# One fused VectorE instruction per head for distance and row maximum, and a single PSUM bank for the values, in the attention of a two-layer encoder

## The chip, the core and the metric

The kernel runs on one core of one Trainium2 chip. The metric is the device time of one execution in microseconds (us). A core has five engines, each with an instruction queue of its own, worked through in order: TensorE (PE: matmuls and transposes, results to the accumulator memory PSUM; PEld is its loading of the stationary operand), VectorE (DVE), ScalarE (ACT), GpSimd (POOL) and SyncE (SP, which here issues most of the DMAs). They meet through semaphores. PSUM has eight banks of 128 partitions x 512 fp32 numbers.

## The reference

Two layers, each of feed-forward, mixer, feed-forward, with a residual and a LayerNorm behind each; the mixer of the first layer is an mLSTM, that of the second the attention that the change touches. 256 tokens, width 1024, 16 query heads of 64 in 4 groups that share keys and values.

```python
def window_attention(x, w_in, sink, w_out):
    """GQA where each query sees keys with |t-s| <= WINDOW, ALiBi bias, per-head sink logit; banded blocks."""
    ...
    s = jnp.einsum('bnqkgd,bnskd->bnkgqs', q, kw).astype(jnp.float32) * (HEAD_DIM ** -0.5)
    ...
    s = s - slopes[:, :, None, None] * dist
    s = jnp.where(valid[None, :, None, None], s, MASK_VALUE)
    ...
    m = jnp.maximum(jnp.max(s, axis=-1, keepdims=True), sink_l)
    pe = jnp.exp(s - m)
    attn = pe / (jnp.sum(pe, axis=-1, keepdims=True) + jnp.exp(sink_l - m))
    o = jnp.einsum('bnkgqs,bnskd->bnqkgd', attn, vw.astype(jnp.float32)).reshape(B, S, nq)
    return o.astype(x.dtype) @ w_out
```

## The kernel before

**Numbers in two parts.** Every operand of a matmul is held as two tiles, hi (rounded to the type fp32r) and lo (the rest). A product is three matmuls, hi x hi, hi x lo and lo x hi (`mm3`, L467). The hi part is made by ScalarE, the lo part by VectorE, for weights (`w_hi`, `w_lo`) as for results that leave PSUM (`split_evac`).

**Weights.** `Weights` (L141) holds a plan of weight pieces in the order of their use. Raw pieces of 512 KB are loaded by SP into four buffers; `high` casts one (ScalarE), `low` subtracts (VectorE) and then loads the next into the buffer that came free. In the attention the call `W.done(..., PU[st], True)` lets at most `PU[st]` pieces be cast in stage `st`, and `W.lows()` makes their low parts.

**Order.** Nothing is reordered (`manual_schedule`): each engine gets its instructions in the order of the Python code. Each instruction of PE, DVE and ACT is recorded by one helper, so that they all show as L132 in the profile and are told apart by the names of their tiles.

**The attention** (`attn`, L1083). POOL first fills constants, zeroes `kp` and computes `dist`, the distance of each query and key (1e33 outside the window). The projections of keys, values and the first queries follow (`proj`, `k_turn`, `q_turn`); the remaining queries are 32 small steps (`q_rest`). Queries are scaled by 1/slope of their head, so scores and distance have one scale. Then eight pairs of heads j go through a pipeline of eleven stages `st` (L1277):

- `scores(j)` in stage j, for each half t of the queries: three matmuls of 512 columns (two heads x 256 keys) and a fourth that adds -1 x `dist`, into one PSUM bank; VectorE takes the row maxima of both heads in one `reduce_max` (`rm`). Then `nm` = -slope x `rm`, and the smaller of that and -sink. ScalarE takes four exponentials from PSUM (`sc`), each with its row sum (an instruction that reads the accumulator follows each), and two small ones of the sink (`es`).
- `scale(j)` in stage j+1, on POOL: the normaliser (a sum, a power of -1) and four scalings of `sc`.
- `turn(j, 0)` and `turn(j, 1)` in stage j+2: four transposes each into a bank, ScalarE's copy `pr_hi`, and later (`flush`) VectorE's `pr_lo`. In stages 2 to 7 the second turn stands behind the matmuls of `scores`.
- `values(j)` in stage j+3: the stationary operand is the two parts of the values side by side, 64 + 64 columns; four matmuls of 512 columns, so that each half of the partitions holds one part's product. ScalarE copies two quarters of the bank (`o`), VectorE adds the other two, and `qT[j]` takes the sum (`q_hi`, `q_lo`).
- What else PE has to do (`fill`): in stages 0 to 3 the steps of `q_rest` between the entries of `QC`, in stages 4 to 10 the output projection `out_proj(st - 4)`, at the end of the stage.

Four PSUM banks (`pw`) serve scores, turns and values in turn; the second turn of a stage uses the bank that the stage's `values` had. Behind the loop the output projection of pair 7 and of the second half of the tokens follows (`tail`), and LayerNorm.

Of the kernel before, what the change touches and what calls it, by code (L numbers as in the profile page):

```python
# [9 lines left out]
F32 = mybir.dt.float32  # L10
FR = mybir.dt.float32r
# [14 lines left out]
S_RAW = 6  # L26
V_RAW = 2
RING = 10
PU = [3, 1, 2, 1, 1, 1, 1, 1, 0, 1, 1, 2]
QC = [5, 16, 22, 27, 32]  # L30
SW = 1
CT = [0, 1]
LC = [1, 0, 0, 0, 0, 1]
TD = [0, 3, 2, 0, 2, 2]
# [280 lines left out]
def trunk_kernel(ctx: ExitStack, tc: tile.TileContext, x, ffn_w_in, ffn_w_out, ln_g, ln_b, ml_w_in, ml_gate_b,  # L315
# [151 lines left out]
    def mm3(o, l, r, start, stop, onto=False):  # L467
        nc.tensor.matmul(o, l[0], r[0], start=start, stop=False, skip_group_check=onto)
        nc.tensor.matmul(o, l[0], r[1], start=False, stop=False, skip_group_check=onto)
        nc.tensor.matmul(o, l[1], r[0], start=False, stop=stop, skip_group_check=onto)  # L470

    def pair(p, *idx):
        return p[0][idx], p[1][idx]
# [9 lines left out]
    def tok(t):  # L483
        return slice(t * 128, (t + 1) * 128)

    def split_evac(dst, src, scale=None):
        if scale is None:
            nc.scalar.copy(dst[0], src)
            nc.vector.tensor_sub(dst[1], src, dst[0].bitcast(F32))
        else:  # L490
            nc.scalar.activation(dst[0], src, AF.Copy, scale=scale)
            nc.vector.scalar_tensor_tensor(dst[1], src, scale, dst[0].bitcast(F32), op0=OP.mult, op1=OP.subtract)
# [590 lines left out]
    def attn(l, n, pending, last):  # L1083
        with ExitStack() as ph:
# [3 lines left out]
            def both(shape, name, bufs=1):  # L1088
                return tuple(tile_(shape, FR, name + e, bufs=bufs) for e in ("_hi", "_lo"))

            minus_one = tile_([128, 32], F32, "minus_one")[:, 0:4].rearrange("p (t a) -> p t a", t=2)
            nc.gpsimd.memset(minus_one, -1.0)
            slope = [2.0 ** (-(h + 1) / 2) for h in range(16)]
            neg_slope = tile_([128, 16], F32, "neg_slope")
            for h in range(16):
                nc.gpsimd.memset(neg_slope[:, h:h + 1], -slope[h])
            qs_row = tile_([128, 8], F32, "qs_row")
            qs_col = tile_([128, 4], F32, "qs_col")
            for h in range(8):
# [7 lines left out]
            for d, sign in ((fwd, 1), (back, -1)):  # L1107
# [4 lines left out]
                                        channel_multiplier=sign)  # L1112
                nc.gpsimd.affine_select(d, d, pattern=[[-128 * sign, 2], [sign, S]], compare_op=OP.is_ge, fill=1e33,
                                        base=128, channel_multiplier=-sign)
            dist = tile_([128, 2, S], FR, "dist")
            nc.gpsimd.tensor_add(dist, fwd, back)
            va = [tile_([128, 4, 2, 64], FR, f"v{t}") for t in range(2)]
            qT = both([128, 8, S], "q")
            kd, qd = [], []

# [2 lines left out]
            def proj(t, m):  # L1123
                ps = wbank()
                for k in range(8):
                    if t == 0 and m == 1 and k == PEND[bound[0] - 1]:
                        pending()
                        W.done(0, PD[bound[0] - 1])
                    if 4 * m + k // 2 == len(pieces):
                        pieces.extend(W.take(1))  # L1130
                    mm3(ps, pair(xT, A, k, tok(t)), pair(pieces[4 * m + k // 2], A, k % 2), k == 0, k == 7)
                    if t == 1 and k % 2:
                        W.done(W.used - 8 + 4 * m + k // 2 + 1, 1 if m == 0 and k < 4 else 0)
                if m == 0:
                    kv = ps.rearrange("p (a g d) -> p a g d", a=2, g=4)
                    kk = tile_([128, 4, 2, 64], F32, "kd", tag="sc", bufs=6)
                    nc.scalar.copy(kk, kv[:, 0, :, None, :].to_broadcast([128, 4, 2, 64]))
                    split_evac((va[t][:, :, 0], va[t][:, :, 1]), kv[:, 1])
                    kd.append(kk)
                else:  # L1140
                    qq = tile_([128, 4, 128], F32, "qd", tag="sc", bufs=6)
                    nc.vector.tensor_mul(qq.rearrange("p j (a d) -> p (j a) d", a=2),
                                         ps.rearrange("p (h d) -> p h d", h=8),
                                         qs_row[:, :, None].to_broadcast([128, 8, 64]))
                    qd.append(qq)
# [39 lines left out]
            def scores(j, between):  # L1185
                g = j // 2
                rm = tile_([128, 2, 2], F32, "rm", bufs=3)
                nm = tile_([128, 2, 2], F32, "nm", bufs=3)
                sm = tile_([128, 2, 2], F32, "sm", bufs=3)
                es = tile_([128, 2, 2], F32, "es", bufs=3)  # L1190
                wide_ = lambda v: v[:, None, 2 * j:2 * j + 2].to_broadcast([128, 2, 2])
                if SW:
                    p1 = wbank((128, 2, S))
                    ps = [wbank((128, 2, S)), p1]
                else:
                    ps = [wbank((128, 2, S)), wbank((128, 2, S))]
                for t in range(2):
                    p = ps[t]
                    mm3(p, pair(qT, A, j, tok(t)), pair(kp, A, g), True, False)
                    nc.tensor.matmul(p, neg_id, dist[:, t, None, :].to_broadcast([128, 2, S]), start=False, stop=True)  # L1200
                    nc.vector.reduce_max(rm[:, t], p, axis=AX.X)
                nc.vector.tensor_mul(nm, rm, wide_(neg_slope))
                nc.vector.tensor_tensor(nm, nm, wide_(neg_sink), op=OP.min)
                if between is not None:
                    between()
                for t in range(2):
                    s_ = tile_([128, 2, S], F32, "sc", bufs=6)
                    for a in range(2):
                        nc.scalar.activation(s_[:, a], ps[t][:, a], AF.Exp, bias=nm[:, t, a:a + 1],
                                             scale=slope[2 * j + a], accum_out=sm[:, t, a:a + 1])  # L1210
                    sc[j, t] = s_
                for a in range(2):
                    nc.scalar.activation(es[:, :, a], nm[:, :, a], AF.Exp, bias=sink[:, 2 * j + a:2 * j + a + 1])
                stat[j] = sm, es
# [19 lines left out]
            lows, sums = [], {}  # L1234

            def values(j):
                p = wbank((128, 2, S))
                for e in range(2):
                    for sb in range(2):
                        v = va[sb][:, j // 2].rearrange("p a d -> p (a d)")  # L1240
                        nc.tensor.matmul(p, v, pr[j, sb][e], start=e == sb == 0, stop=e == sb == 1)
                o = tile_([128, S], F32, "o", bufs=2)
                top, low = slice(0, 64), slice(64, 128)
                nc.scalar.copy(o[top], p[top, 0])
                nc.scalar.copy(o[low], p[low, 1])
                nc.vector.tensor_add(o[top], p[low, 0], o[top])
                nc.vector.tensor_add(o[low], p[top, 1], o[low])
                sums[j] = o

            y = []  # L1250

            wo = {}

            def out_proj(c, toks):
                if not y:
                    y.extend([ybank() for _ in range(2)] for _ in range(2))
                if c not in wo:
                    wo[c], = W.take_rows(1)
                for t in toks:
                    for o in range(2):  # L1260
                        mm3(y[t][o], pair(qT, A, c, tok(t)), pair(wo[c][1], A, 0, slice(o * 512, o * 512 + 512)),
                            c == 0, False)

            proj(0, 0)
            proj(0, 1)
# [11 lines left out]
            for st in range(11):  # L1277
                if st == 2:
                    gb = load_ln(lambda name: tile_([128, D], F32, name), l, n)
                if 0 <= st - 3 < 8:  # L1280
                    values(st - 3)
                if 0 <= st - 1 < 8:
                    scale(st - 1)
                late = None
                if 0 <= st - 2 < 8:
                    p0, p1 = wbank((128, 2, S)), wbank((128, 2, S))
                    turn(st - 2, 0, p0)
                    late = lambda: turn(st - 2, 1, p1)
                    if st >= 8 or not SW:
                        late()  # L1290
                        late = None
                if 0 <= st - 3 < 8:
                    o = sums.pop(st - 3)
                    d = pair(qT, A, st - 3)
                    nc.scalar.copy(d[0], o)
                    lows.append((d, o))
                held = [wo[c][0] for c in wo if c not in CT]
                W.done(min([W.used - (2 if qpart else 0)] + held), PU[st], True)
                if st < 8:
                    scores(st, late)  # L1300
                flush(3)
                W.lows()
                if st in fill:
                    f_, *args = fill[st]
                    f_(*args)
            nc.scalar.preload_act_table(AF.Silu)
            W.done(0, PU[11])
            wo[7], = W.take_rows(1)
# [46 lines left out]
```

## Time and profile before

| | us |
|---|---|
| median of 3 runs | 941.51 (940.34 to 942.21) |
| the profiled execution | 940.93 |
| its span, first to last instruction | 939.2 |
| PE busy | 923.1 (98%) |
| DVE busy | 800.5 (85%) |
| ACT busy | 546.6 (58%) |
| the loop over pairs of heads, about | 685 to 744 |

TensorE's granted clock is 0.999 of full speed. Matmuls are pipelined: a row's duration (0.39 us for 512 columns) is longer than the step from one start to the next (0.227 us), so TensorE can show as busy while it waits a little. A row of the groups reads: line, engine, operation, output<-inputs by name, partitions x elements and type, count | busy us, mean ns of one | idle time of the engine just before them, and what ended most of it.

### The profile page before, as it was taken

Reading aid. Unit: us, or ns where it says so; the run is one execution under the profiler, and the core shown is the slowest. Engines: PE = TensorE matmul, PEld = TensorE weight load, DVE = VectorE, ACT = ScalarE, POOL = GpSimd, SP = SyncE. Lnnn points to the kernel's source line nnn. Section 1 sums busy time; section 2 is a strip of 40 time slices with the busy share of each in tenths; the row PEclk is TensorE's granted clock in tenths of the full one; section 3 lists DMA queues with packets and bytes.
Section 4 is the critical chain, followed back from the end, with each engine's and each line's share of the span. In section 5 each row is a group of like instructions: output and inputs, shape, how many; then the busy total and the mean of one; then the engine's idle time right before and its main releaser. Section 6 shows DMA issues by size and latency. Waiting matters only on the chain.

```text
span 939.2 us, 12338 instructions
## 1 busy us (share of the span) xinstructions
PE 923.1 (98%) x4416; PEld 765.2 (81%) x4416; DVE 800.5 (85%) x943; ACT 546.6 (58%) x781; POOL 103.2 (11%) x162
## 2 busy tenths in 40 slices
PE   8999999999999999999999999999999999999996
PEld 7888888889878788888888888887887788888885
DVE  6899998787697799988888899977878888898975
ACT  5666756347563548565535566563678554757460
POOL 2010101011111000101010101010545300000100
PEclk9999999999999999999999999999999999999999
DMA  8979764546434949695559597746543266769531
GB/s 277 353 189 326 224 225 89 203 134 219 163 119 145 311 143 336 170 323 135 174 160 347 126 326 210 247 90 201 178 141 109 68 223 248 229 219 311 162 87 45
DMA packets 98461, 187.54 MB, mean 200 GB/s; under 512 B 6720, under 2 KB 37456, under 8 KB 98400
## 3 DMA queue, kind: packets, MB, share of 16 engines
q1 hardware_dynamic: 91648, 174.09, 53.7%
q0 software_dynamic: 6752, 12.66, 8.3%
q8 instruction: 35, 0.57, 0.2%
q14 instruction: 26, 0.21, 0.1%
HBM read 185.68 MB, written 1.05 MB: 199 GB/s over the span
## 4 chain that ended last, share of the span: by engine, by line
PE 84%; DVE 7%; ACT 3%; DMA 2%; issue 2%; POOL 1%; SPq 1%; DVEq 0%; ACTq 0%
PE pw L132 55%; PE py L132 29%; DVE w_lo L132 2%; DMA s_raw<-in_ffn_w_in_dram 1%; ACT w_hi L132 1%; DMA w_raw<-in_ffn_w_in_dram 1%; ACT sc L132 1%; DVE h L132 1%; DVE x L132 1%; DMA w_raw<-in_ml_w_in_dram 0%; SPq L98 0%; DVE o L132 0%; DVE rm L132 0%; DVE pr_lo L132 0%; DVE wt L132 0%
## 5 line engine op out<-in xcount | busy, mean ns | idle before, releaser
L132 DVE TENSOR_TENSOR w_lo<-w_raw,w_hi 128x1024 fp32r<-128x1024 f32 (+1 forms) x237 | 280.8, 1216 | 17.6 <-ACT w_hi L132 15.5
L132 ACT CAST w_hi<-w_raw 128x1024 fp32r<-128x1024 f32 (+1 forms) x237 | 240.6, 1049 | 72.9 <-DMA w_raw<-in_ffn_w_in_dram 21.7
L132 PE MATMUL pw<-w_hi,xT_hi 128*128 128x512 f32 x560 | 222.4, 397 | 0.3 <-ACT xT_hi L132 0.3
L132 PE MATMUL pw<-w_hi,xT_lo 128*128 128x512 f32 x560 | 218.8, 391 | 0.0
L132 PE MATMUL pw<-w_lo,xT_hi 128*128 128x512 f32 x560 | 218.2, 390 | 0.1
L132 ACT CAST w_hi<-s_raw 128x1024 fp32r<-128x1024 f32 x144 | 148.3, 1051 | 92.2 <-DVE s_raw L132 56.4
L132 DVE TENSOR_TENSOR w_lo<-s_raw,w_hi 128x1024 fp32r<-128x1024 f32 x144 | 172.6, 1219 | 21.4 <-ACT w_hi L132 21.3
L132 PE MATMUL py<-w_hi,h_hi 128*128 128x512 f32 x352 | 138.1, 392 | 0.3 <-ACT h_hi L132 0.3
L132 PE MATMUL py<-w_hi,h_lo 128*128 128x512 f32 x352 | 137.3, 390 | 0.2 <-DVE h_lo L132 0.2
L132 PE MATMUL py<-w_lo,h_hi 128*128 128x512 f32 x352 | 137.1, 390 | 0.0
L132 PEld LDWEIGHTS pw<-w_hi,xT_lo 128*128 128x128 f32 x560 | 105.1, 188 | 23.3 <-DVE xT_lo L132 0.8
L132 PEld LDWEIGHTS pw<-w_lo,xT_hi 128*128 128x128 f32 x560 | 105.3, 188 | 20.8 <-DVE w_lo L132 0.4
L132 PEld LDWEIGHTS pw<-w_hi,xT_hi 128*128 128x128 f32 x560 | 105.2, 188 | 20.7 <-ACT xT_hi L132 0.7
L132 DVE TENSOR_TENSOR s_raw<-s_raw 128x1024 f32<-128x1024 f32 x72 | 87.0, 1219 | 0.7
L261 POOL DMA_DIRECT2D s_raw<-in_ffn_w_in_dram x24 | 29.0, 1209 | 496.4 <-DVE w_lo L132 378.3
L132 PEld LDWEIGHTS py<-w_hi,h_lo 128*128 128x128 f32 x352 | 66.1, 188 | 15.1 <-DVE h_lo L132 1.4
L132 PEld LDWEIGHTS py<-w_hi,h_hi 128*128 128x128 f32 x352 | 66.1, 188 | 13.9 <-ACT h_hi L132 0.7
L132 PEld LDWEIGHTS py<-w_lo,h_hi 128*128 128x128 f32 x352 | 66.1, 188 | 13.7 <-DVE w_lo L132 0.4
L132 PE MATMUL pw<-w_hi,S_hi 128*128 128x512 f32 x192 | 74.7, 389 | 0.0
L132 PE MATMUL pw<-w_hi,S_lo 128*128 128x512 f32 x192 | 74.7, 389 | 0.0
L132 PE MATMUL pw<-w_lo,S_hi 128*128 128x512 f32 x192 | 74.7, 389 | 0.0
L132 DVE TENSOR_TENSOR h_lo<-pw,h_hi 128x512 fp32r<-128x512 f32 x44 | 30.2, 687 | 23.3 <-ACT h_hi L132 23.0
(218 smaller groups left out, 1114.1 us busy)
## 6 DMA issues: line engine op xcount, KB each, us to landing
w_raw<-in_ffn_w_out_dram SPq DMA_DIRECT2D x88, 512.0 KB, 5.3
s_raw<-in_ffn_w_in_dram SPq DMA_DIRECT2D x72, 512.0 KB, 6.0
w_raw<-in_ffn_w_in_dram SPq DMA_DIRECT2D x56, 512.0 KB, 5.0
w_raw<-in_ffn_w_in_dram SPq DMA_DIRECT2D x96, 256.0 KB, 4.4
s_raw<-in_ffn_w_in_dram POOLq DMA_DIRECT2D x24, 512.0 KB, 5.9
w_raw<-in_ml_w_in_dram SPq DMA_DIRECT2D x24, 512.0 KB, 4.5
w_raw<-in_at_w_in_dram SPq DMA_DIRECT2D x12, 512.0 KB, 4.5
w_raw<-in_ml_w_out_dram SPq DMA_DIRECT2D x8, 512.0 KB, 3.6
```

Of the source, the lines that this page charges most:

```text
L132: r = f(out, *args, **kw)
L261: nc.gpsimd.dma_start(t.rearrange("p (k f) -> p k f", k=self.words[w]["k"]), v, accum_op=OP.add)
```

## The change

The distance leaves the matmuls. `scores` has three matmuls of 512 columns per half; then, for each head, one VectorE instruction reads the scores from PSUM and `dist` from SBUF, writes their difference to `sc` in SBUF, and takes its row maximum, which starts from sink/slope (`sink_max`, made by POOL), so that the separate minimum with -sink goes. In the built program each such instruction is followed by one that reads its accumulator into `rm`. The exponentials read `sc` and not PSUM. Between the halves of the queries one waiting `pr_lo` is made (`flush(1)`).

The values lie between zeros: a tile has five columns of 64 per group (zero, hi, zero, lo, zero), filled by POOL beforehand. A window of 128 columns that begins on a zero column or on a part puts one head's product into the upper or the lower half of the partitions and zero into the other, so both heads, both token blocks and the three products hi x hi, lo x hi and hi x lo sum up in one bank of 256 columns with twelve matmuls. (The product lo x lo, which the four matmuls before held too, is left out.) `o` is gone; `qT` is read from that bank at once, ahead of the turns.

The fill work can be split: `FB[st]` of its parts come before the first turn of the stage. `QC` and `PU` are shifted by one at some places.

```diff
-PU = [3, 1, 2, 1, 1, 1, 1, 1, 0, 1, 1, 2]
-QC = [5, 16, 22, 27, 32]
+PU = [2, 1, 2, 1, 1, 1, 1, 1, 0, 1, 1, 2]
+QC = [4, 16, 21, 27, 32]
+FB = [1, 0, 2, 3, 0, 0, 0, 0, 1, 1, 0]
...
-            dist = tile_([128, 2, S], FR, "dist")
+            dist = tile_([128, 2, S], F32, "dist")
             nc.gpsimd.tensor_add(dist, fwd, back)
-            va = [tile_([128, 4, 2, 64], FR, f"v{t}") for t in range(2)]
+            for h in range(16):
+                nc.gpsimd.memset(sink_max[:, h:h + 1], 1.0 / slope[h])
+            nc.gpsimd.tensor_tensor(sink_max, sink_max, sink, op=OP.mult)
+            va = [tile_([128, 4, 5, 64], FR, f"v{t}") for t in range(2)]
+            for t in range(2):
+                nc.gpsimd.memset(va[t][:, :, 0:5:2].bitcast(F32), 0.0)
...
-                    split_evac((va[t][:, :, 0], va[t][:, :, 1]), kv[:, 1])
+                    split_evac((va[t][:, :, 1], va[t][:, :, 3]), kv[:, 1])
...
-                    mm3(p, pair(qT, A, j, tok(t)), pair(kp, A, g), True, False)
-                    nc.tensor.matmul(p, neg_id, dist[:, t, None, :].to_broadcast([128, 2, S]), start=False, stop=True)
-                    nc.vector.reduce_max(rm[:, t], p, axis=AX.X)
+                    mm3(p, pair(qT, A, j, tok(t)), pair(kp, A, g), True, True)
+                    sc[j, t] = tile_([128, 2, S], F32, "sc", bufs=6)
+                    for a in range(2):
+                        nc.vector.tensor_tensor_reduce(sc[j, t][:, a], p[:, a], dist[:, t], 1.0,
+                                                       sink_max[:, 2 * j + a:2 * j + a + 1], OP.subtract, OP.max,
+                                                       rm[:, t, a:a + 1])
+                    if t == 0:
+                        flush(1)
                 nc.vector.tensor_mul(nm, rm, wide_(neg_slope))
-                nc.vector.tensor_tensor(nm, nm, wide_(neg_sink), op=OP.min)
...
-                        nc.scalar.activation(s_[:, a], ps[t][:, a], AF.Exp, bias=nm[:, t, a:a + 1],
+                        nc.scalar.activation(s_[:, a], s_[:, a], AF.Exp, bias=nm[:, t, a:a + 1],
                                              scale=slope[2 * j + a], accum_out=sm[:, t, a:a + 1])
...
-                p = wbank((128, 2, S))
-                for e in range(2):
-                    for sb in range(2):
-                        v = va[sb][:, j // 2].rearrange("p a d -> p (a d)")
-                        nc.tensor.matmul(p, v, pr[j, sb][e], start=e == sb == 0, stop=e == sb == 1)
-                o = tile_([128, S], F32, "o", bufs=2)
-                top, low = slice(0, 64), slice(64, 128)
-                nc.scalar.copy(o[top], p[top, 0])
-                nc.scalar.copy(o[low], p[low, 1])
-                nc.vector.tensor_add(o[top], p[low, 0], o[top])
-                nc.vector.tensor_add(o[low], p[top, 1], o[low])
-                sums[j] = o
+                p = wbank((128, S))
+                terms = [(sb, a, e, f) for sb in range(2) for e, f in ((0, 0), (1, 0), (0, 1)) for a in range(2)]
+                for n_, (sb, a, e, f) in enumerate(terms):
+                    v = va[sb][:, j // 2].rearrange("p s d -> p (s d)")
+                    at = 128 * e + 64 * (1 - a)
+                    nc.tensor.matmul(p, v[:, at:at + 128], pr[j, sb][f][:, a], start=n_ == 0, stop=n_ == len(terms) - 1)
+                sums[j] = p
...
                 if 0 <= st - 3 < 8:
                     values(st - 3)
+                    o = sums.pop(st - 3)
+                    d = pair(qT, A, st - 3)
+                    nc.scalar.copy(d[0], o)
+                    nc.vector.tensor_sub(d[1], o, d[0].bitcast(F32))
                 if 0 <= st - 1 < 8:
                     scale(st - 1)
                 late = None
+                work = parts(*fill[st]) if st in fill else []
                 if 0 <= st - 2 < 8:
+                    for f_ in work[:FB[st]]:
+                        f_()
+                    work = work[FB[st]:]
                     p0, p1 = wbank((128, 2, S)), wbank((128, 2, S))
                     turn(st - 2, 0, p0)
...
-                if 0 <= st - 3 < 8:
-                    o = sums.pop(st - 3)
-                    d = pair(qT, A, st - 3)
-                    nc.scalar.copy(d[0], o)
-                    lows.append((d, o))
...
-                flush(3)
+                flush(2)
                 W.lows()
-                if st in fill:
-                    f_, *args = fill[st]
-                    f_(*args)
+                for f_ in work:
+                    f_()
```

`parts` turns the stage's `q_rest` into its single steps, and its `out_proj` into one part per token half and output half, three matmuls of 512 columns each. In this order a `q_rest` step is three matmuls of 256 columns.

More of the change, by code (lines that the diff above doesn't have):

```diff
@@ L1089, in both @@
                 return tuple(tile_(shape, FR, name + e, bufs=bufs) for e in ("_hi", "_lo"))
-            minus_one = tile_([128, 32], F32, "minus_one")[:, 0:4].rearrange("p (t a) -> p t a", t=2)
+            minus_one = tile_([128, 16], F32, "minus_one")[:, 0:4].rearrange("p (t a) -> p t a", t=2)
             nc.gpsimd.memset(minus_one, -1.0)
@@ L1096, in attn @@
                 nc.gpsimd.memset(neg_slope[:, h:h + 1], -slope[h])
+            sink_max = tile_([128, 16], F32, "sink_max")
             qs_row = tile_([128, 8], F32, "qs_row")
@@ L1206, in scores @@
                 for t in range(2):
-                    s_ = tile_([128, 2, S], F32, "sc", bufs=6)
+                    s_ = sc[j, t]
                     for a in range(2):
-                        nc.scalar.activation(s_[:, a], ps[t][:, a], AF.Exp, bias=nm[:, t, a:a + 1],
+                        nc.scalar.activation(s_[:, a], s_[:, a], AF.Exp, bias=nm[:, t, a:a + 1],
                                              scale=slope[2 * j + a], accum_out=sm[:, t, a:a + 1])
-                    sc[j, t] = s_
                 for a in range(2):
@@ L1236, in values, with out_part @@
             def values(j):
-                p = wbank((128, 2, S))
-                for e in range(2):
-                    for sb in range(2):
-                        v = va[sb][:, j // 2].rearrange("p a d -> p (a d)")
-                        nc.tensor.matmul(p, v, pr[j, sb][e], start=e == sb == 0, stop=e == sb == 1)
-                o = tile_([128, S], F32, "o", bufs=2)
-                top, low = slice(0, 64), slice(64, 128)
-                nc.scalar.copy(o[top], p[top, 0])
-                nc.scalar.copy(o[low], p[low, 1])
-                nc.vector.tensor_add(o[top], p[low, 0], o[top])
-                nc.vector.tensor_add(o[low], p[top, 1], o[low])
-                sums[j] = o
+                p = wbank((128, S))
[5 more added lines that the diff above has]
+                sums[j] = p
             y = []
             wo = {}
-            def out_proj(c, toks):
+            def out_part(c, t, o):
                 if not y:
@@ L1258, in out_proj, with parts @@
                     wo[c], = W.take_rows(1)
+                mm3(y[t][o], pair(qT, A, c, tok(t)), pair(wo[c][1], A, 0, slice(o * 512, o * 512 + 512)), c == 0, False)
+            def out_proj(c, toks):
                 for t in toks:
                     for o in range(2):
-                        mm3(y[t][o], pair(qT, A, c, tok(t)), pair(wo[c][1], A, 0, slice(o * 512, o * 512 + 512)),
-                            c == 0, False)
+                        out_part(c, t, o)
+            def parts(f_, *args):
+                if f_ is q_rest:
+                    return [lambda i=i: q_rest([i]) for i in args[0]]
+                return [lambda t=t, o=o: out_part(args[0], t, o) for t in args[1] for o in range(2)]
             proj(0, 0)
```

## The prediction

> **What bounds the kernel now.** I read the page first: its chain that ended last, and the busy time of stretches around the attention.
>
> ```profile
> PE 84%; DVE 7%; ACT 3%; DMA 2%; issue 2%; POOL 1%; SPq 1%; DVEq 0%; ACTq 0%
> ```
>
> ```profile
> 686.00:724.00 38.00, 36.40 (x210) 30.65 (x211) 32.40 (x58) 32.59 (x94) 19.99 (x34) 1.00 0.43 143
> 724.00:744.00 20.00, 18.71 (x89) 13.29 (x88) 17.09 (x33) 16.28 (x44) 7.60 (x15) 1.00 0.26 83
> 744.00:764.00 20.00, 20.00 (x97) 16.67 (x96) 17.64 (x23) 7.96 (x10) 3.06 (x2) 1.00 0.32 100
> ```
>
> The columns after the stretch and its length are PE, PEld, DVE, ACT and POOL busy. The kernel as a whole is bound by TensorE, at full clock. The loop over eight pairs of heads, 685 to 744 us, is the exception: VectorE and ScalarE are each busy for some 85% of it and TensorE waits. To see by how much, I went through TensorE's timeline there and took from each start the step that an unhindered matmul of its kind needs (512 columns 0.227 us, 256 columns 0.12, a 128-column transpose 0.089). The waits left over, above 0.1 us each, come to some 7 us. That is all that a change to this loop can win from TensorE. The chain of waits shows one late turn of the loop:
>
> ```profile
> 726.57 1.54 PE pw L132 x5
> ...
> 728.17 0.36 ACT o L132
> ...
> 728.94 0.43 DVE o L132
> ...
> 729.83 1.30 DVE rm L132 x2
> ...
> 731.15 0.17 DVE nm L132
> ...
> 731.77 1.93 ACT sc L132 x8
> ```
>
> The columns are start, length, what. ScalarE copies a finished sum of values, VectorE adds its halves, then takes the row maxima of the next pair, and only then can ScalarE start that pair's exponentials. Those start, pair 0 to 7, at 689.23, 695.31, 700.59, 707.38, 713.36, 719.54, 725.98 and 731.77, and the first matmul behind the loop at 743.36, 11.59 after the last. These nine marks are what I follow below.
>
> **The change part by part.** Rows for the prices, from the groups by shape:
>
> ```profile
> L132 DVE TENSOR_TENSOR_SCAN fm<-ones,ig 32x256 f32<-32x256 f32 x2 | 1.4, 678 | 0.0
> ...
> L132 DVE TENSOR_REDUCE rm<-pw 128x2 f32<-128x512 f32 x16 | 10.5, 687 | 2.5 <-PE pw L132 2.4
> L132 DVE SCALAR_TENSOR_TENSOR q_lo<-py,qs_col,q_hi 128x256 fp32r<-128x256 f32 x4 | 1.8, 477 | 0.1
> L132 ACT ACTIVATION_READ_ACCUMULATOR sc<-pw,nm 128x1 f32 x32 | 6.5, 203 | 0.0
> L132 DVE TENSOR_TENSOR o<-pw,o 64x256 f32<-64x256 f32 x16 | 6.8, 422 | 4.3 <-ACT o L132 4.0
> ```
>
> *TensorE.* Per pair two 512-column distance matmuls go (2 x 0.227) and the values' four of 512 become twelve of 256: 12 x 0.12 - 4 x 0.227 = +0.53. Net +0.08 us, over eight pairs +0.6 us. It lies on the path only where TensorE is not waiting.
>
> *VectorE.* Per pair the two reductions (1.30 start to start) and one of two small products of 0.16 to 0.2 go, and both half adds (0.86). Four fused instructions come, each followed, in the program as built, by one that reads its accumulator. The trace has no such pair; call its cost, start to start, p. Below: 256 elements from PSUM with a per-partition scalar take 477 ns and step 0.39 us when two follow each other, and a 128x1 instruction (rs, 154 ns) lets the next one start after 0.07: 0.46. Floor of all bounds: the plain 256-element step without scalar, 0.34, plus 0.07 = 0.41. Above: the half-rate scan, 678 ns on 256 elements, with the read unhidden (154): 0.83. Nearest in kind is ScalarE's own pair: its 256-element exponential (473 ns) plus the 203 ns read steps 0.45 us, against 0.37 for its scaled copies of the same size with no read (two h in 0.84). So the read adds 0.08 and 0.39 + 0.08 = 0.47; I take p = 0.48.
>
> [...]
>
> *ScalarE.* The exponentials now read SBUF; the row e<-e takes 633 ns where g<-pw from PSUM takes 599, so +0.034 x 4 = +0.14 us per pair. Two copies of half sums (0.75) and the cast of o (0.41) become one cast of 256 from PSUM (0.38, as v<-pw).
>
> *The loop* from one pair's exponentials to the next, as built: exponentials 2.19 + 0.14, cast 0.40, low part of q 0.44, four fused pairs 4p, between them a low part of the weights 0.62 (it sits behind the first two fused pairs now), product and hand-over 0.28. That is 4.07 + 4p = 5.99, against 5.79 measured before (725.98 to 731.77). Where a query evacuation of q_rest comes in, +0.43. So the loop itself gains nothing.
>
> *Walk with p = 0.48.* Pair 0: scores and VectorE are ready at 686.92; + 4p + 0.28 = 689.1. Pair 1: + 2.33, two query casts 1.07, a low part 0.45, 4p + 0.28 = 695.15. Pair 2 hangs on ScalarE: + 2.33, a weight cast 0.55, two 1024-wide casts 2.0, another 0.55 = 700.6. Pair 3 hangs on VectorE: behind pair 2's second weight cast a low part 0.65, two 1.18 splits, two low parts of q 0.84, then 4p + 0.90: 707.2. Pairs 4 and 5 follow at 713.6 and 719.6. Pair 6: TensorE is full from the bank that pair 3's low part frees (3.6 after 707.2): turn 0.36, out_proj 2.75, values 1.44, turn 0.36, scores 1.4, and again turn, out_proj, values, turn and 0.97 to the first scores, 12.2, then 4p + 0.90: 725.8. Pair 7: + 5.99 = 731.8. So all eight marks lie within 0.25 us of before.
>
> *Behind pair 7* the gain appears. Its exponentials 2.33; normaliser and scalings on POOL 3.53 with the hand-over (734.15 to 737.60 before, unchanged); the last turn until its first half can be evacuated 0.38; one cast and two low parts 1.85; the last value matmuls 0.3; six matmuls of out_proj(6) 1.45: 9.85, against 11.59. TensorE reaches the turns of stages 8 and 9 with one part of out_proj more behind it (FB), where it waited 0.25 to 0.5, so it is not what ends last there. Before, values(7) was followed by copies, adds and a cast (0.75 + 0.86 + 0.41) in front of the first tail matmul, which waited 0.91 for q_hi; now by one cast that out_proj(6) hides. 731.8 + 9.85 = 741.65 against 743.36: **-1.7 us**.
>
> *Moves that cost nothing, and their cover.* POOL's new set-up (16 small fills 0.59, a product at most 1.04, two 128x768 fills of about 0.7 by the 128x1024 row's 0.95) runs behind dist, 681.2 to 684.3; the first fused instruction comes at 686.9, the zeros are read at 699, POOL's next job at 691.6. Uncovered it would be 3.0 us. The next weight splits come one stage later (PU), and the queue of SP sends one 512 KB load of at_w_out behind the two norm loads; that row is read over 30 us later, and the next stage's first weights at 753.9, ten us after the last split. One query group moves behind the scores of pair 0 and one behind those of pair 2: TensorE idles 0.36 us more at 685.4, where it waits for kp_lo anyway, and gets the work back. The two groups of 0.36 now ahead of the first turn fill its wait for POOL (0.78). The fused instruction's destination sc, six buffers, is free: pair j-3 was turned a stage before.
>
> Sensitivity: 4p lies on the path for about six pairs, so 0.01 on p is 0.24 us; break-even near p = 0.55. The profiled execution was 940.93, 1.73 over its span of 939.2, and 0.6 under the median of 941.51 that I add to: 941.51 - 1.7 = 939.8 (span near 937.5).
>
> **The rivals.**
> 1. *TensorE takes the loop back.* If p is 0.41, the waits at 707 to 709, 726 to 728 and 732 to 734 close too and TensorE binds from pair 4 on: only about 16p counts, -1.7 - 16 x 0.07 = -2.8, and with the joints of stages 8 and 9 closed some 0.7 more: 938.0. For it: those waits are all on VectorE's low parts. Against: it needs both the scalar and the read almost free.
> 2. *The fused instruction runs at half rate.* Then it costs what the scan does, p = 0.68 - 0.09 (the overlap that 0.477 against 0.39 shows) + 0.08 = 0.67. 0.19 x 24 = 4.6 on the path, -1.7 + 4.6 = +2.9: 944.4, slower. It decides from p = 0.55 and reaches 0.2% at 0.63. For it: the scan is VectorE's only row with two tensors in and a value carried from element to element. Against: the plain reduction carries one too, and takes 512 elements in 687 ns.
> 3. *The read waits until the fused instruction has drained.* p = 0.477 + 0.07 = 0.55: the loop's loss eats the tail's gain, 941.6. ScalarE's read, which starts 0.1 us before its exponential ends, speaks against.
> 4. *The change does not free what it means to.* The bank of the scores comes free at the maximum and not at the exponential, but no matmul waits for that bank by name; if the last stages hang on POOL more than I see, the tail keeps 11.3 and the time is 941.2.
>
> **How the numbers follow.** 0.2% is 1.9 us, about what a measurement of this kernel can tell from no change: 939.6 and 943.4. Forecast (p 0.45 to 0.52, -2.4 to -0.7): 0.46, a little under half of it below 939.6. Rival 1: 0.16. Rival 2: 0.16. Rivals 3 and 4: 0.22 together, a tail of 0.06 of it slower. Faster 0.21 + 0.16 + 0.03 = 0.40; slower 0.16 + 0.06 + 0.02 = 0.24; same 0.36. The likeliest one's own range is 939.0 to 941.0. The range for 8 in 10 runs from 937.2, a little past rival 1, to 944.8, past rival 2's middle.
>
> **What would show it.** Right: fused rows near 0.47 us that step 0.48 with their read; exponentials of pairs 3 to 7 within 0.5 us of the marks; the first tail matmul 9.9 to 10.2 after pair 7, with no wait for q_hi. Wrong: fused rows of 0.6 or more, a turn waiting for q_lo for over 0.5 us in several stages, or a tail that still waits.

## The result

| | before | after |
|---|---|---|
| median of 16 runs each, taken side by side, us | 941.44 (940.34 to 943.20) | 940.33 (937.80 to 942.62) |
| ratio, 95% interval | 1 | 0.9984 (0.9977 to 0.9991) |
| profiled execution / its span, us | 940.93 / 939.2 | 940.39 / 938.7 |

By the ratio the kernel became 0.16% faster, about 1.5 us (0.8 to 2.2); the medians lie 1.1 us apart. That is close to the 1.7 us forecast, but not by the terms of the forecast, as the traces and twelve further kernels show.

The span fell by 0.5 us only. The trace of after reaches the cast `kp_hi` that opens the second turn of keys 1.05 us later than that of before, through code that the change doesn't touch (TensorE is 1.39 late already at its 400th instruction, far ahead of the attention); in the 14 traces of this study this cast lies anywhere between 682.33 and 686.35 us. So below I use a **stretch** inside each trace, from that cast (683.37 in before, 684.42 in after) to the first matmul of `out_proj(7)` behind the loop (743.36 and 742.52). It is 59.99 us before and **58.10** after, 1.89 less. (Behind it after takes 0.34 us more; with the 1.05 that leaves 0.5 of the 1.89 in the span.) The expectations' "first cast kp_hi" with 59.99 means the same cast.

### The profile page after: what moved, and what is told of

It is laid out like the page before. It is cut to its first block, busy times and chain, and to the rows that moved or that the text cites. A ratio compares the mean times of both kernels' runs of the same rounds, so it can differ in the third digit from the quotient of the medians.

```text
span 938.7 us, 12456 instructions
## 1 busy us (share of the span) xinstructions
PE 923.0 (98%) x4464; PEld 768.6 (82%) x4464; DVE 795.3 (85%) x967; ACT 542.9 (58%) x765; POOL 103.0 (11%) x181
## 3 DMA queue, kind: packets, MB, share of 16 engines
HBM read 185.68 MB, written 1.05 MB: 199 GB/s over the span
## 4 chain that ended last, share of the span: by engine, by line
PE 76%; DVE 11%; ACT 4%; DMA 4%; issue 3%; POOL 1%; SPq 0%; DVEq 0%; ACTq 0%; POOLq 0%
PE pw L133 47%; PE py L133 28%; DVE w_lo L133 5%; DMA w_raw<-in_ffn_w_in_dram 2%; ACT w_hi L133 2%; DMA w_raw<-in_ffn_w_out_dram 1%; DVE s_raw L133 1%; DMA s_raw<-in_ffn_w_in_dram 1%; ACT sc L133 1%; DVE x L133 1%; DVE h L133 1%; ACT S_hi L133 0%; DVE S L133 0%; DVE e L133 0%; DVE sc L133 0%
```

## The profile after

The first two of the stretches that the prediction shows (columns as there: PE, PEld, DVE, ACT, POOL):

```profile
686.00:724.00 38.00, 36.26 (x237) 31.97 (x236) 30.30 (x81) 31.07 (x88) 17.13 (x33) 1.00 0.42 132
724.00:744.00 20.00, 19.81 (x121) 16.77 (x120) 15.06 (x35) 14.47 (x36) 7.90 (x16) 1.00 0.26 75
```

From 724 to 744 us TensorE went from 18.71 to 19.81 of 20 us, while VectorE and ScalarE each lost some 2 us of work. That is the end of the loop and the tail, where the forecast put the gain. (In after, too, a row of 512 columns lasts 0.39 us and steps 0.23, so a short wait can hide in TensorE's busy time, and the next views go by starts.) The prices of the new instructions, from the groups by shape, and their order on VectorE, from the timeline (start, length, instruction):

```profile
L133 ACT ACTIVATE sc<-sc,nm 128x256 f32<-128x256 f32 x32 | 15.9, 499 | 8.1 <-DVE nm L133 8.1
L133 DVE CUSTOM_DVE_ANT_0 sc<-pw,dist,sink_max 128x256 f32<-128x256 f32 x32 | 14.0, 479 | 2.1 <-PE pw L133 1.7 <-POOL sm L1229 0.4
...
L133 ACT ACTIVATION_READ_ACCUMULATOR sc<-sc,nm 128x1 f32 x32 | 6.0, 188 | 0.0
```

```profile
688.07 0.48 DVE L133 CUSTOM_DVE_ANT_0 sc<-pw,dist,sink_max 128x256 f32<-128x256 f32 x1 [0.28 <-PE pw L133]
688.48 0.08 DVE L133 DVE_READ_ACCUMULATOR2_ANT rm<- 128x1 f32 x1
688.48 0.48 DVE L133 CUSTOM_DVE_ANT_0 sc<-pw,dist,sink_max 128x256 f32<-128x256 f32 x1
```

The read of the accumulator and the next fused instruction start at the same time: the read costs nothing, and the fused instruction steps 0.405 us. The exponentials from SBUF take 499 ns and step 0.49, against 473 and 0.45 before. The chain of waits through the loop (start, length, what):

```profile
705.80 0.60 DVE pr_lo L133
706.41 0.39 DVE sc L133
...
706.81 0.40 DVE sc L133
...
707.53 1.54 ACT sc L133 x6
...
710.77 0.43 DVE q_lo L133
...
711.24 0.66 PE pw L133 x4
711.90 2.75 PE py L133 x12
714.64 3.70 PE pw L133 x26
718.34 2.75 PE py L133 x12
721.09 3.49 PE pw L133 x24
...
724.71 0.60 DVE pr_lo L133
...
729.63 0.66 PE pw L133 x4
730.29 1.39 PE py L133 x6
...
739.74 1.56 PE pw L133 x12
```

Three things stand there. The low part `pr_lo`, which the change puts between the fused instructions, lies on the chain twice. (It is the low part of the attention's own weights; the expectations call it a low part of the weights. `w_lo` is that of the layer's weights.) At 711.24 TensorE's second turn has waited for `q_lo`: its bank is the one that `values` wrote, and is free only when `q_lo`, behind the exponentials and a cast on ScalarE, has read it (1.01 us over the nominal step from 710.00). And from 711 to 724.6 TensorE alone sets the time, as again from 729.63 to the end. The former is not new, though the forecast did not use it. The chain of before is TensorE's too, from 707.92 to 728.11:

```profile
707.92 3.71 PE pw L132 x16
...
712.32 2.77 PE py L132 x12
715.09 3.65 PE pw L132 x20
718.74 2.77 PE py L132 x12
721.51 3.65 PE pw L132 x20
725.17 1.40 PE py L132 x6
```

The same marks as in the prediction, counted from the start of the stretch:

| us | pair 0 | 1 | 2 | 3 | 4 | 5 | 6 | 7 | end | end behind pair 7 |
|---|---|---|---|---|---|---|---|---|---|---|
| before | 5.86 | 11.94 | 17.22 | 24.01 | 29.99 | 36.17 | 42.61 | 48.40 | 59.99 | 11.59 |
| after | 5.65 | 11.55 | 16.75 | 23.11 | 29.27 | 35.54 | 41.99 | 47.88 | 58.10 | 10.22 |

Of the 1.89 us, 0.90 are won up to pair 3, 0.38 given back up to pair 7, and 1.37 won behind it.

## The experiments

Each kernel was timed over five rounds against the kernel before on the same chip.

| kernel | ratio to before (95%) | stretch, us |
|---|---|---|
| after | 0.9984 (0.9977 to 0.9991) | 58.10 |
| e1 values part only | 1.0006 (0.9995 to 1.0018) | 60.63 |
| e2 fused part only | 1.0033 (1.0021 to 1.0045) | 62.51 |
| e10 fused part only, low parts behind | 1.0006 (0.9997 to 1.0015) | 59.88 |
| e3 order of fills as before | 0.9991 (0.9981 to 1.0000) | 58.65 |
| e4 a fifth fused instruction | 0.9979 (0.9968 to 0.9991) | 58.88 |
| e5 difference in PSUM | 0.9995 (0.9986 to 1.0004) | 58.86 |
| e8 two more matmuls per pair | 1.0005 (0.9997 to 1.0014) | 59.51 |
| e6 part ahead, stages 4 and 7 | 0.9978 (0.9968 to 0.9988) | 57.35 |
| e7 part ahead, stages 4 to 7 | 0.9973 (0.9962 to 0.9983) | 57.41 |
| e9 low parts behind | 0.9971 (0.9959 to 0.9984) | 56.58 |
| e11 e7 and e9 | 0.9972 (0.9958 to 0.9986) | 56.42 |
| e12 e9, one split moved | 0.9954 (0.9941 to 0.9967) | 56.27 |

The intervals are about 1 us wide to each side, so differences below that are read from the stretch. It comes from one trace per kernel; the marks of pairs 0 and 1 in after, e6, e7, e9 and e11, ahead of what differs in these, agree within 0.03 us.

### The two halves of the change, each alone (e1, e2)

e1 puts the scores of before back into the changed kernel:

```diff
-                    mm3(p, pair(qT, A, j, tok(t)), pair(kp, A, g), True, True)
...
-                        nc.vector.tensor_tensor_reduce(sc[j, t][:, a], p[:, a], dist[:, t], 1.0,
...
-                        flush(1)
+                    mm3(p, pair(qT, A, j, tok(t)), pair(kp, A, g), True, False)
+                    nc.tensor.matmul(p, neg_id, dist[:, t, None, :].to_broadcast([128, 2, S]), start=False, stop=True)
+                    nc.vector.reduce_max(rm[:, t], p, axis=AX.X)
```

> The new values path (twelve matmuls of 256 columns into one bank, one cast, one low part) with the old scores (distance as a matmul, maximum by reduction, exponentials from PSUM). Stretch meant below: from the first cast kp_hi to the first matmul of out_proj(7), 59.99 us in the trace of before, 58.10 in that of after. Theory (the gain sits behind the loop, in the path of o, and the fused maximum only pays for TensorE's extra 0.53 us per pair): the tail behind pair 7's exponentials stays near 10.2 us (11.59 before), but TensorE carries 0.45 us more per pair than in after and binds in the two stages with whole out_proj parts, so some 0.5 to 0.9 of the gain is lost: stretch 58.6 to 59.2, time 0.3 to 1.0 us under before. Rival 1 (the fused instruction brings the gain, by its 0.405 us): stretch 60 or more, time as before or up to 2 us slower. Rival 2 (the fused half costs time, the values half alone is better): stretch under 58.1.

e2 keeps the fused scores and puts back the values tile without zeros, the four matmuls, the copies and adds of `o` and its late cast.

> The fused subtract and maximum, exponentials from SBUF, with the old values (four matmuls of 512 columns, two copies, two half adds, a late cast of o); fills, query groups and weight splits placed as in after. Theory: the tail behind pair 7 goes back to 11.3 to 11.6 us; the loop costs four fused instructions 1.62 plus four exponentials 0.18 dearer against 1.30 and 0.18 before, so +0.3 us per pair on the three or four pairs where VectorE sets the turn, less some 0.5 for the covered wait for POOL: stretch 60 to 60.8 us, time 0 to 0.8 us over before. Rival 1 (the fused instruction brings the gain): stretch 58.1 to 58.8, time 1 us or more under before. Rival 3 (the two halves add up): what this run gains or loses and what the values half alone gains add up to after's 1.9 us of the stretch within 0.3.

e1 comes out at 60.63, 0.64 longer than before: neither half alone wins. Theory had the direction (the halves need each other), but put e1 under before; rival 1's number is the nearer one, though its reason is not, as e2 shows. The chain of e1 says what holds it:

```profile
710.36 4.41 PE pw L133 x28
714.76 2.77 PE py L133 x12
717.54 4.16 PE pw L133 x28
721.70 2.77 PE py L133 x12
724.47 4.17 PE pw L133 x28
```

From 710.36 to 734 us, and again from 735.9 on, it is all TensorE, with 28 matmuls and transposes and 4.16 us where after has 26 and 3.70: the two distance matmuls. e2, at 62.51, is the other failure, far worse than expected. Its chain over one pair:

```profile
713.04 1.89 ACT sc L133 x7
...
715.76 0.38 ACT o L133
...
716.60 0.42 DVE o L133
...
717.54 0.40 DVE sc L133
717.95 0.60 DVE pr_lo L133
718.55 0.39 DVE sc L133
718.95 0.40 DVE sc L133
...
719.64 1.89 ACT sc L133 x7
```

No TensorE at all: ScalarE and VectorE form a closed ring of 6.60 us (719.64 - 713.04), which repeats for pairs 4 to 7, against 5.79 before. Rival 3 (the halves add up) is out: +0.64 and +2.52 against -1.89 together.

### What the removed matmuls are worth to TensorE (e8)

```diff
+                    nc.tensor.matmul(p, qT[0][:, j, tok(t)], kp[0][:, g], start=True, stop=True)
                     mm3(p, pair(qT, A, j, tok(t)), pair(kp, A, g), True, True)
```

> The changed kernel with two more 512-column matmuls per pair, each ahead of a half's scores in the same bank and overwritten by them: TensorE's work of the removed distance matmuls (0.454 us per pair) without any of their other effects. Theory (TensorE sets the loop from pair 3 to 6 and behind pair 7, so the worth of the fused part is the matmuls it removes, and the values part can't have its own gain without it): the stretch grows from 58.10 to 59.5 to 60.2, near the 60.60 of the values part alone, and the gain of after is gone: within 0.5 us of before. Rival (VectorE's and ScalarE's chain sets the loop and TensorE has idle time to hide them): under 58.7.

59.51 and 1.0005: TensorE's 0.454 us per pair, put back without anything else, costs 1.41 us of the stretch, and in time the whole gain is gone. e1, which lacks the fused part, is longer than after by 2.53, so 1.12 are not explained by e8 alone. An account of TensorE's time explains both. The matmuls and transposes in the stretch, counted in the traces and priced by the prediction's steps (0.227, 0.12 and 0.089 us), leave a rest that is TensorE's waiting and what single steps take beyond these (called waiting below):

| us of the stretch | matmuls and transposes | rest |
|---|---|---|
| before | 51.4 | 8.6 |
| e1 values part only | 55.6 | 5.0 |
| e10 fused part only, low parts behind (below) | 47.8 | 12.1 |
| after | 52.0 | 6.1 |
| e8 two more matmuls per pair | 55.6 | 3.9 |

The values part takes 3.6 us of waiting away and brings 4.3 of matmuls; the fused part takes 3.6 of matmuls away and brings 3.5 of waiting. Together the waiting falls by 2.5 for 0.6 of matmuls. So the fused part's worth lies on TensorE, where it pays for the values' 0.53 per pair. Of e8's 3.6 us, 2.2 fill what was waiting. e1 has the same matmuls as e8, and its 1.12 more are waiting.

### What VectorE's price is worth (e4) and where the low part stands (e9, e10)

e4 runs the last fused instruction of a pair a second time, into tiles that nobody reads.

> The changed kernel with a fifth fused instruction per pair, the last one a second time into tiles that nobody reads: 0.405 us more of VectorE per pair, as if each of the four had cost 0.506 instead of 0.405. Forecast's slope (VectorE's instruction lies on the path for six pairs, 0.24 us per 0.01 of its cost): +2.4 us, stretch 60.5. Theory after the trace (it lies on the path only for pairs 1, 3 and 6, or 7, where the chain of waits names it, and TensorE or ScalarE sets the other turns): +1.0 to +1.6, stretch 59.1 to 59.7. Rival (TensorE has taken the loop): under +0.5.

58.88: 0.405 us more per pair cost 0.78, which is 1.9 pairs' worth, not six. By the marks it counts at pairs 0, 3 and 4 (+0.26, +0.28, +0.29 over after) and at no later pair. The theory's 1.0 to 1.6 was still too high; the time can't tell e4 from after. e9 moves the low part `pr_lo`, 0.6 us, out from between the fused instructions:

```diff
-                    if t == 0:
-                        flush(1)
...
-                flush(2)
+                flush(3)
```

> The changed kernel without the low part of the weights between the first and the second two fused instructions: both low parts follow the product, as before the change. Stretch: from the first cast kp_hi of the second turn of keys to the first matmul of out_proj(7), 59.99 in before, 58.10 in after. Theory (what VectorE does ahead of the maximum counts at pairs 3 and 7 alone, as the fifth fused instruction showed; the low part of the second turn, which values waits for last, ends at the same time either way): the exponentials of pair 3 start 0.4 to 0.6 earlier, the stretch is 57.5 to 57.9. Rival (the low part of the first turn, 1 us later now, is what TensorE waits for: its bank and the first values matmuls hang on it): TensorE waits longer for pr_lo, stretch 58.1 or more.

> The fused part alone (run e2, stretch 62.51) with the low parts of the weights behind the product, as before the change. In e2 the exponentials of pairs 4 to 7 follow each other by 6.6 us, a closed ring of ScalarE and VectorE. Theory (that ring is the one of before, 5.79, plus four exponentials 0.16, fused against reduced 0.32, the low part put between 0.60, less one small product 0.16, 6.71): without the low part the period falls to 6.0 to 6.2 and the stretch to 60.3 to 61.2. Rival 1 (the low part was not in the ring): period within 0.15 of 6.6. Rival 2 (it falls below 5.8, so that fused instructions cost less than the reductions): stretch under 59.5.

In e10, the same edit on e2, the period of pairs 4 to 7 falls from 6.6 to 6.19, 6.18 and 6.02 us: the low part was in the ring, as the theory said. The stretch of 59.88 lies under the 60.3 to 61.2 expected; without the low part in the ring the fused part alone neither wins nor loses. On the whole change the edit brings 1.52 us (56.58), beyond the theory's range: pair 3 starts 0.51 earlier, the wait for `q_lo` shrinks from 1.01 to 0.31, and pair 7 starts 1.86 earlier. The chain of e9 is TensorE's alone from 710.11 to the end of the stretch, where after has VectorE and ScalarE in it once more, at pair 6:

```profile
710.11 0.66 PE pw L133 x4
710.77 2.77 PE py L133 x12
713.53 3.69 PE pw L133 x26
717.23 2.75 PE py L133 x12
719.98 3.70 PE pw L133 x26
723.68 1.39 PE py L133 x6
```

With the low parts behind in all four kernels, the two halves now read: values alone +0.64, fused alone -0.11, both -3.41. (All three have the new order of the fills, which the next run prices in after only.) By the marks, the gain up to pair 3 is the fused half's (24.01 in before, 24.11 in e1, 23.14 in e10) and the gain behind pair 7 is the values half's (11.59, 11.00 and 11.99).

### The order of the fills (e3)

`FB = [0] * 11`, `PU` and `QC` as before the change.

> The changed kernel with the order of the work around it as before: no part of a fill ahead of a turn (FB all zero), query groups split as before (QC), the third weight split in the first stage (PU). Theory: TensorE's wait for POOL's normaliser ahead of the first turn (0.78 us before, gone in after) comes back for some 0.5 us, and the waits of 0.25 to 0.5 at the turns of stages 8 and 9 too: stretch 58.8 to 59.6, time 0.7 to 1.5 over after. Rival: those waits were covered anyway, because ScalarE and VectorE set these turns: stretch within 0.3 of 58.1, time that of after.

58.65, between the theory and the rival, a little nearer the theory: 0.15 us of it from pair 1 on (TensorE waits 1.39 for POOL at the first turn, but most of that is covered), 0.40 behind pair 7 (0.62 us of waiting in stage 9). In time it is 0.7 us, within the intervals.

### TensorE's wait for the low part of q (e6, e7, e11)

```diff
+                    ahead = work[:1] if st in (4, 7) else []
+                    work = work[len(ahead):]
-                    late = lambda: turn(st - 2, 1, p1)
+                    late = lambda: ([f_() for f_ in ahead], turn(st - 2, 1, p1))
```

> The changed kernel with one part of out_proj put between the scores and the late turn in stages 4 and 7, where TensorE waits 1.01 and 0.36 us for q_lo of the same stage (the turn writes the bank of the values that q_lo reads last). Theory (this wait is new, it is what the change gives back, and TensorE sets the time from there to pair 6): 0.69 of work fills the wait, and the stretch falls from 58.10 to 57.2 to 57.5, time 0.6 to 0.9 under after. Rival (the turn's casts and low parts come later by as much and hold up the next stage): stretch within 0.25 of 58.10.

> As e6, with one part ahead of the late turn in each of the stages 4 to 7. In stages 5 and 6 TensorE does not wait there. Theory: as e6 within 0.3, since the turn has about 1 us of slack before the exponentials that follow its cast on ScalarE. Rival (no slack): 0.5 or more longer than e6.

(e7 has `range(4, 8)` for `(4, 7)`.) 57.35 and 57.41, both as the theory had it: the wait cost 0.75 us. It is less new than the expectation says. In before TensorE waits 0.92 us over the nominal step for the same bank one stage earlier (705.37, for the half adds `o`), but the chain goes by VectorE there; new is that the wait lies on the chain. With e9's edit it is nearly gone already, so both together bring only 0.16 more than e9:

> The kernel with one part of out_proj ahead of the late turn in stages 4 to 7 (stretch 57.41) and, besides, the low parts behind the product. Theory: with TensorE's wait filled, VectorE's chain ends last at more pairs, so the low part's 0.6 counts at pairs 3, 6 and 7: stretch 56.4 to 57.0, time 0.4 to 1.0 under that kernel and 2.5 to 3.5 under before. Rival (TensorE waits for the low part instead): stretch 57.3 or more.

The stretch, 56.42, is at the edge of what was expected, and the time, 2.6 us under before, inside it; against e7 alone (0.9973) the ratio of 0.9972 shows nothing of the 0.4 to 1.0 us expected, which the intervals would hide.

### The exponentials' source (e5)

The fused instruction's output is `p[:, a]` and not `sc[j, t][:, a]`, and the exponentials read `ps[t]`.

> The changed kernel with the fused instruction's difference written back into its PSUM bank, so that the exponentials read PSUM again. Theory: one exponential steps 0.45 us instead of 0.495, 0.18 per pair; VectorE and ScalarE set the turn only for pairs 0, 3 and 7, so the stretch (58.10 in after) loses 0.3 to 0.6: 57.5 to 57.8. Rival 1 (a write to PSUM is dearer for VectorE): the fused row grows from 479 ns and steps more than 0.45; by e4, where 0.405 per pair cost 0.78 of the stretch, 0.05 on each of the four costs 0.4 and the gain is gone: 58.0 to 58.6. Rival 2 (the bank matters that is now held until the exponential and not until the maximum, some 2 us longer): a turn or a score waits for ACT sc by name, stretch over 58.6.

58.86: the theory fell, and rival 1 holds by a price larger than it named. The exponentials do get cheaper (477 ns instead of 499), but the timeline of VectorE shows:

```profile
711.66 0.48 DVE L133 CUSTOM_DVE_ANT_0 pw<-pw,dist,sink_max 128x256 f32<-128x256 f32 x1
712.06 0.14 DVE L133 DVE_READ_ACCUMULATOR2_ANT rm<- 128x1 f32 x1
712.23 0.49 DVE L133 CUSTOM_DVE_ANT_0 pw<-pw,dist,sink_max 128x256 f32<-128x256 f32 x1
712.64 0.14 DVE L133 DVE_READ_ACCUMULATOR2_ANT rm<- 128x1 f32 x1
712.64 0.69 DVE L133 TENSOR_TENSOR pr_lo<-pw,pr_hi 128x512 fp32r<-128x512 f32 x1
```

The read is no longer hidden from the second instruction of the same bank, which starts 0.57 us behind the first; a `pr_lo` behind it still starts together with the read (712.64). The built program says why. In e5 each of the 16 second instructions waits for a semaphore that the read ahead of it raises (the read ends at 712.20 here, and the instruction starts at 712.23); in after none of them does. Twice 0.17 us per pair, 0.34, is near e4's 0.405, and the stretch is that of e4. Rival 2's sign is there too, but small: the weight loads of TensorE wait for `ACT sc` 0.19 and 0.24 us at two places, and pair 0 is 0.42 late already, before any bank is taken again.

### A version that beats both (e12)

```diff
-PU = [2, 1, 2, 1, 1, 1, 1, 1, 0, 1, 1, 2]
+PU = [2, 1, 1, 1, 1, 1, 1, 1, 1, 1, 1, 2]
```

on top of e9.

> The changed kernel with the low parts of the weights behind the product (run e9, stretch 56.57, 0.9971 of before) and one of the two weight splits of stage 2 moved to stage 8, where ScalarE is mostly idle (PU). In e9 the product of pair 2 is ready at 699.3 and its exponentials start at 700.53, behind two weight casts of 1.0 us each on ScalarE. Theory (as the forecast had it, pair 2 hangs on ScalarE's casts): pair 2's exponentials start 0.8 to 1.0 earlier, pair 3's by 0.5 to 1.0, TensorE binds behind that, stretch 55.6 to 56.1, time 0.5 to 1.0 under e9. Rival 1 (TensorE's turn or values hold pair 3): pair 2 earlier, pair 3 not, stretch within 0.2 of 56.57. Rival 2 (the moved split is late for the next stage's first weights): the stretch shrinks, but TensorE waits for w_hi or w_lo behind it and the time does not.

Pair 2 starts 0.95 earlier and pairs 3 to 7 0.70, as the theory said, but the end only 0.31: 0.4 comes back as a new wait behind pair 7, where the chain goes through POOL.

```profile
731.98 1.03 POOL sm L1227
...
733.10 2.82 POOL sc L1230 x4
...
735.96 0.77 PE pw L133 x5
```

So the stretch of 56.27 misses the expected 55.6 to 56.1. At 0.9954 (0.9941 to 0.9967) e12 is faster than before, and its interval lies below that of after; against e9 the intervals overlap.

## Why the prediction was right, and where its steps were not

**"The loop itself gains nothing", "behind pair 7 the gain appears": half right.** The tail gained 1.37 (10.22 where 9.85 was forecast, no wait for `q_hi`). Its end is not set by POOL and the casts, as the sum had it, but by TensorE's backlog: the chain is PE alone from 729.63 on. The loop gained 0.52 at pair 7, where the marks were forecast unchanged. A loop 0.5 better and a tail 0.4 worse than forecast make nearly the sum that was forecast: that the total came so close is luck. At the 0.2% by which the forecast parts faster from same, 0.16% is the same.

**p = 0.48: mis-sized.** It is 0.405, below the floor of 0.41. The step that failed is "so the read adds 0.08", taken from ScalarE's pair of instructions. VectorE's read is hidden whole. Rival 3, the read that waits, is what e5 shows under another condition (0.57 us from the first to the second instruction of a bank).

**"4p lies on the path for about six pairs", 0.24 us per 0.01: the step that failed most.** e4 measures 0.78 us for 0.101 on p, 0.08 per 0.01. The forecast counted VectorE for six turns although its own walk had TensorE full at pair 6, and although the chain of before is TensorE's from 707.92 to 728.11. This error hid most of the one in p: by the forecast's slope, p = 0.405 would have brought 1.8 us more (0.075 x 24), and the time would have been near 938; by the measured slope it brings 0.6.

**The low part "behind the first two fused pairs", 0.62: right in size.** It was taken as given in the ring. e9 shows that this placement alone gives back 1.52 us.

**A turn waiting for `q_lo`:** named as a sign of trouble for several stages. It came in one (1.01 us) and a little in another (0.36), and cost 0.75 (e6). It is also why rival 1's time did not come although its p did: at p = 0.405 TensorE binds from pair 4 to pair 6, but behind a loop that arrives late. With the wait and the low part out of the way (e11) the ratio is 0.9972, 938.8 on the median of before, near rival 1's 938.0.

**Net +0.08 us for TensorE per pair:** right, and more important than it seemed. A late stage of the chain takes 3.70 + 2.75 us on TensorE in after and 3.65 + 2.77 in before. It balances two terms of 0.45 and 0.53, each of which decides when it stands alone (the 0.53 on before in e1, the 0.45 on after in e8).

**Exponentials +0.034 each:** 0.04 in the step (0.49 against 0.45), small. **FB "fills its wait for POOL":** credited nothing, it brought 0.55 with `QC` and `PU` (e3), most of it behind pair 7. **Rival 2, half rate, 0.67:** out: with the scores in PSUM and `dist` in SBUF the rows take 479 ns and step 0.405, where the scan, from which it was worked out, takes 678 ns for as many elements. **Rival 4:** out, the tail is 10.22 and not 11.3.

## What to carry to other kernels

When a loop is held by two limits at about the same height, a change that relieves one and loads the other, and its mirror image, can each be worth nothing alone and something together; test the halves before crediting either. A price counts only for the turns where its engine ends last, so multiply by the turns that the chain names and not by all of them. After a change that moves an evacuation or shortens a stage, look at once for the instruction that is now in the way: here one low part between two maxima and one turn behind a bank were worth 1.68 us of the stretch together (e11), nearly as much as the change's own 1.89.

## What the runs showed of the hardware

- VectorE's read of an accumulator behind a fused subtract and maximum of 256 elements cost nothing where the difference went to SBUF (after: 82 ns, the next instruction starts with it, step 0.405 us). Where source and destination were the same PSUM bank, it took 0.14 us, the next instruction on that bank waited for its semaphore, and the step was 0.57 us (e5). The longer step is thus the wait that the program carries; why the read itself takes 0.14 us is open.
- ScalarE's exponential of 256 elements with a row sum took 499 ns and stepped 0.49 us from SBUF (after), 473 to 477 ns and 0.45 from PSUM (before and e5): 0.04 us less from one start to the next.
